# Output gates' weight tiles split two deep into two rings; LN1's second transposes moved forward, residual offset added in the second chunk

## The chip, the cores and the metric

The kernel runs on one core of a Trainium2 chip. The metric is the device time of one execution in microseconds (us); the kernel before takes 890.56 us, the median of three runs (889.98 to 890.59).

## The reference, cut to what matters

One layer of a decoder with a batch of 1, 512 tokens, a model width of 1024 and a hidden width of 4096, all in fp32. A token mixer runs gated linear attention (GLA, 4 heads, chunks of 64 tokens) and latent attention (MLA, 8 heads) side by side, merges them by sigmoid gates and projects the sum. Then comes a squared-ReLU MLP. Each half is a residual step followed by a LayerNorm, with alpha = 2^0.25:

```
h  = layer_norm(x, ln_in)
q_g, k_g, v_g, r_g, a_lr, q_lat, kv_lat, gate_logits = split(h @ w_in)
y_gla = (rms_norm(o_gla) * silu(r_g)) @ w_o_gla
y_mla = merge_heads(o_mla) @ w_o_mla
mix = (g_gla * y_gla + g_mla * y_mla) @ w_out
h1  = layer_norm(alpha * h + mix, ln1)            # LN1
ff  = square(relu(h1 @ w_ff1)) @ w_ff2
out = layer_norm(alpha * h1 + ff, ln2)
```

The change touches r_g (the output gates of GLA, a product of 512 x 1024 by 1024 x 1024), LN1, and alpha * h1, which enters LN2. Since h1 = n * g + b for the normalised rows n, the residual is n * (alpha g) + alpha b: one multiply by a row and one add of a row (the "offset").

## The kernel before, in words

**Products.** Every fp32 number that enters TensorE is split in two: hi, its rounding to the type fp32r, and lo, the rest. A product is the sum of three matmuls, hi by hi, hi by lo and lo by hi (L245 to L247 in gemm_fm, L279 to L281 in gemm_tm). In gemm_fm the weights stand still and the activations stream through, so the lo part of the weights (wlo) is used by every third matmul.

**Weights.** All weights pass through one list, `stream`, in the order of use. An entry is a tile of 128 x 1024 numbers, 512 KB. `fetch` issues an entry's DMA on SP's queue, two entries ahead, into one of three buffers named wraw. `pump` splits it: hi on ACT (L189, an activation that copies), lo on DVE (L190, a subtract). An entry is split at most "ahead" entries before its use (1 if nothing else is said), into the rings that its "home" names: "w" is two whi and two wlo buffers, "r" is two of the three wraw buffers, "a" is the large pool. A ring's buffer can be written again only when the matmuls that read its last content are through.

**Order.** Each engine works its instructions off in order and waits for semaphores of the others. The order is set when the program is built: work that runs beside the products is written as generators (`spawn`, `tick`, `finish`), and a list scheduler with estimated costs then orders each engine's instructions. `tc.issue_after(x)` ties the instructions inside it to stand behind x in that order; where x is on another engine it adds a wait.

**Output gates (proj_r, L701 to L761, 145 to 184 us).** The product is computed by a Strassen-like scheme with seven products, in the order 11, 21, t2, t1, t3, 22, t4 (RW), each with two halves of its inner dimension: 14 tiles of `stream`, 12 matmuls of 128 x 512 each (L746 to L748). The tiles 11, 21 and 22 are loaded by SP into wraw. The t tiles are sums of weights that are formed in DRAM-to-SBUF loads (r_load, and r_acc on POOL's queue, which adds in the DMA); they stand in buffers named wq and are split from there ("src"). The last, t4, is made by r_acc4 (L763), two accumulating DMAs on POOL's queue, issued after the t1 product. The sums of activations are loaded as xr tiles by SP (x_load, L709). The levels of the GLA run beside the product as generators: POOL multiplies into rp (L786, L787), ACT takes an exponential (E, L792), DVE a mask product (M, L794), and PE small matmuls (L848, L852, L856).

**LN1 (L1340 to L1357, about 545 to 570 us).** ln_rows (L422) gets mean and variance of a row block on DVE, the power -1/2 on POOL (L428), and normalises on DVE (L434, the "affine"). ln_transpose (L436) then handles a half of the tokens (256) in eight steps k: two PE transposes (L443), hi on ACT (L446), and lo on DVE (L450 and L451) or, for odd k, with ACT's help (L448). The first product behind it is f1 of the MLP. For its first weight block it runs over the first token half alone (L1356: eight steps k, each with four groups of three matmuls of 256 columns), while the second half goes through ln1(1); the second token half follows.

**The MLP (from L1507).** The hidden width is worked in four chunks. In a chunk, f1 (gemm_fm, weights in tiles of two k each, so four tiles a block) makes the hidden activations, with ReLU (L1516) and square (L1521) on ACT. win_hid (L1420) makes sums of them, and win_f2 (L1438) multiplies with w_ff2 by a Winograd-like scheme (matmuls L1454 to L1456). Its results are copied to "ev" tiles on ACT (L1471) and added to the residual in SBUF by accumulating DMAs on POOL's queue (res<-ev, L1473). The weights of w_ff2 for the next chunk are loaded on POOL's queue too (win_load, L1393), and their sums T1, T3 and T2 are formed on DVE (win_sums, L1402, operations at L1407). These are tied behind the last ev (st["ev"]), which in the first chunk does not exist yet, so that they are free there.

**The residual (residual1, L1359).** It is spawned after the first block of f1 in the first chunk. ACT's queue loads the two rows ln1_g and ln1_b, broadcast over 128 partitions (bc, 512 KB each, L106). DVE scales both by alpha (L1363, L1364), and then multiplies (L1365, L1369) and adds (L1370) for each of the four row blocks res0 to res3. All of that ends before the first chunk's win_f2 (`finish(t_r1)`).

Of the kernel before, what the change touches and what calls it, by code (L numbers as in the profile page):

```python
# [15 lines left out]
AF = mybir.ActivationFunctionType  # L16
ALU = mybir.AluOpType
AX = mybir.AxisListType

P = 128  # L20
T = 512
D = 1024
NT = T // P
# [12 lines left out]
ALPHA = 2.0 ** 0.25  # L36
# [16 lines left out]
def tile_hybrid_block(ctx: ExitStack, tc: tile.TileContext, I, out, dbg=None):  # L53
    nc = tc.nc
# [41 lines left out]
    act = nc.scalar.activation  # L96
    vtt = nc.vector.tensor_tensor
    vts = nc.vector.tensor_scalar
    stt = nc.vector.scalar_tensor_tensor
    gtt = nc.gpsimd.tensor_tensor  # L100
    mm = nc.tensor.matmul

    def bcast_row(name):
        t = A([P, D], F32, "bc")
        src = I[name]
        nc.scalar.dma_start(t, bass.AP(tensor=src.tensor, offset=src.offset, ap=[[0, P], [1, D]]))  # L106
        return t
# [21 lines left out]
    ident = ca[:, 0:P]  # L129
# [80 lines left out]
    def spawn(g):  # L210
        active.append(g)
        return g
# [19 lines left out]
    def part(x, i, c):  # L232
        return x[i][:, c] if isinstance(x, tuple) else x[:, i, c]

    def gemm_fm(pl, xs, n, evac, width=None, toks=slice(0, T), accs=None, guard=None):
        na = n // P
        accs = accs or [MM() for _ in range(na)]
        for k in range(pl["nk"]):
            hi, lo = weights(pl, k)
            xh, xl = part(xs[k], 0, toks), part(xs[k], 1, toks)  # L240
            first, last = k == 0, k == pl["nk"] - 1
            for a in range(na):
                c = slice(a * P, (a + 1) * P)
                o = accs[a][:, toks]
                mm(o, hi[:, c], xh, start=first, stop=False)  # L245
                mm(o, hi[:, c], xl, start=False, stop=False)  # L246
                mm(o, lo[:, c], xh, start=False, stop=last)  # L247
            if not last:
                tick(width)
        if guard:  # L250
            guard()
        if evac is not None:
            for a in range(na):
                evac(a, accs[a])
                if a == na // 2 - 1:
                    pump(pl["idx"][-1] + 1)
        tick(width)
        return accs
# [41 lines left out]
    PL = {}  # L300
# [16 lines left out]
    for op, _ in RW:  # L317
        for hf in range(2):
            PL["r"].append(len(stream))
            e = {"nk": 2, "n": T, "res": False}  # L320
            if op[0] == "t":
                e["src"] = lambda q=("r", op, hf): WQ[q]
            else:
                e["dmas"] = [(slice(0, 2), r_src(op, hf), None)]
            stream.append(e)
# [96 lines left out]
    def ln_rows(src, dst, mv, on_act=False):  # L422
        bst = S([P, 2, 6], F32, "bst")
        for j in range(2):
            nc.vector.bn_stats(bst[:, j, :], src[:, j * T:(j + 1) * T])
        nc.vector.bn_aggr(mv, bst)
        vts(mv[:, 1:2], mv[:, 1:2], LN_EPS, None, op0=ALU.add)  # L427
        gtt(mv[:, 1:2], mv[:, 1:2], mhalf[:, 0:1], op=ALU.pow)  # L428
        if on_act:
            nmr = S([P, 1], F32, "nmr")  # L430
            stt(nmr, mv[:, 0:1], -1.0, mv[:, 1:2], op0=ALU.mult, op1=ALU.mult)
            act(dst, src, AF.Identity, scale=mv[:, 1:2], bias=nmr)
        else:
            vts(dst, src, mv[:, 0:1], mv[:, 1:2], op0=ALU.subtract, op1=ALU.mult)  # L434

    def ln_transpose(rows, g, b, outs, hf, alt=False, n="h0"):  # L436
        tk = slice(hf * 256, (hf + 1) * 256)
        for k in range(NK):
            if len(outs) <= k:
                outs.append(A([P, 2, T], F32R, n) if n == "h0" else (B([P, T], F32R, n), B([P, T], F32R, n)))  # L440
            p = MM() if alt and k in (4, 5) else PX()
            for i in range(2):
                nc.tensor.transpose(p[:, i * P:(i + 1) * P], rows[2 * hf + i][:, k * P:(k + 1) * P], ident)  # L443
            tmp = B([P, 256], F32, "lnt")
            hi, lo = part(outs[k], 0, tk), part(outs[k], 1, tk)
            ha = act(hi, p[:, :256], AF.Identity, scale=g[:, k:k + 1], bias=b[:, k:k + 1])  # L446
            if (alt or n == "h1") and k % 2:
                act(tmp, p[:, :256], AF.Identity, scale=g[:, k:k + 1], bias=b[:, k:k + 1])  # L448
            else:
                vts(tmp, p[:, :256], g[:, k:k + 1], b[:, k:k + 1], op0=ALU.mult, op1=ALU.add)  # L450
            hd = vtt(lo, tmp, f(hi), op=ALU.subtract)  # L451
            if n == "h1":
                st["ln"] = (ha, hd)
            yield hd
# [466 lines left out]
    scale = HQ ** -0.5  # L921
# [418 lines left out]
    def ln1(hf):  # L1340
        for tt in (2 * hf, 2 * hf + 1):
            mv = S([P, 2], F32, "mv")
            ln_rows(res[tt], res[tt], mv)
        yield
        for k, _ in enumerate(ln_transpose(res, ln1g, ln1b, h1T, hf, n="h1")):
            if k % 2:
                yield
# [5 lines left out]
    finish(t_ln)  # L1353
    st["gates"] = st["ln"]
    t_ln = spawn(ln1(1))
    accs = gemm_fm(PL["f1", 0, 0], h1T, T, None, toks=slice(0, 256))  # L1356
    finish(t_ln)  # L1357

    def residual1():  # L1359
        bg, bb = bcast_row("ln1_g"), bcast_row("ln1_b")  # L1360
        yield
        with tc.issue_after(st["ln"][1].ins):
            vts(bg, bg, ALPHA, None, op0=ALU.mult)  # L1363
            vts(bb, bb, ALPHA, None, op0=ALU.mult)  # L1364
            vtt(res[0], res[0], bg, op=ALU.mult)  # L1365
        yield
        for tt in range(NT):
            if tt:
                vtt(res[tt], res[tt], bg, op=ALU.mult)  # L1369
            vtt(res[tt], res[tt], bb, op=ALU.add)  # L1370
            yield

# [29 lines left out]
    def win_sums(ci):  # L1402
        def held(*a, **kw):
            with ExitStack() as gates:
                if "ev" in st:
                    gates.enter_context(tc.issue_after(st["ev"].ins))
                vtt(*a, **kw)  # L1407
        for hf in range(2):
            q12 = WQ.pop((("f2", ci), ("12", hf)))
            t1 = WQ[("f2", ci), ("T1", hf)] = A([P, 2, T], F32, "T1")  # L1410
            held(t1, q12, WQ[("f2", ci), ("11", hf)], op=ALU.subtract)
            yield
            held(q12, WQ[("f2", ci), ("22", hf)], q12, op=ALU.subtract)
            WQ[("f2", ci), ("T3", hf)] = q12
            yield
            t2 = WQ[("f2", ci), ("T2", hf)] = A([P, 2, T], F32, "T2")
            held(t2, q12, WQ[("f2", ci), ("11", hf)], op=ALU.add)
            yield
# [88 lines left out]
    for ci in range(FC):  # L1507
# [19 lines left out]
        for b, w in F1[ci]:  # L1527
            if ci == 0 and b == 0:
                gemm_fm(PL["f1", ci, b], h1T, T, ev_h, toks=slice(256, T), accs=accs)
                t_r1 = spawn(residual1())  # L1530
            else:
                gemm_fm(PL["f1", ci, b], h1T, w * P, ev_h, width=2)
            if win and b == 0:
                t_ws = spawn(win_sums(ci))
        if ci == 0:
# [107 lines left out]
```

## Time and profile before

| what | value |
|---|---|
| median of 3 runs | 890.56 us (889.98 to 890.59) |
| the profiled execution | 890.77 us |
| its span (first to last instruction on the core) | 888.9 us |
| granted clock of TensorE, mean | 0.999 |
| PE, matmuls | 98% of the span, 4844 instructions |
| PEld, weight loads | 85%, 4844 |
| DVE | 71%, 1011 |
| ACT | 53%, 824 |
| POOL | 20%, 198 |
| instructions | 12959 |
| moved by DMA | 130.92 MB, mean 147 GB/s |

PE is TensorE's matmuls, PEld its weight loads (which overlap them), DVE VectorE, ACT ScalarE, POOL GpSimd, SP SyncE, which here only issues DMAs. The share is busy time over the span; it is an average over stages with different limits. A line of the timeline gives the start in us from the span's start, the duration, the engine and line, the output and inputs by their names in the program, the shape, and how many like instructions it groups; a bracket gives the idle time of the engine before it and what ended it. A group of matmuls such as "f32 x2" has one duration for the whole group. The names L245 and so on are lines of the kernel before.

### The profile page before, as it was taken

The page shows a single profiled execution, that of the slowest core. Times are in us where ns is not written, and L with a number is a line of the kernel's source. Part 1 is how long each engine was busy: PE and PEld are TensorE (multiplying, and loading weights), DVE is VectorE, ACT ScalarE, POOL GpSimd, SP SyncE. Part 2 cuts the span into 40 slices and gives each one's busy share as a digit, 9 for nine tenths or more (in the row PEclk, how much of TensorE's full clock was granted, in tenths as well). Part 3 has the DMA queues.
Part 4 walks back from the last instruction along what each step waited for, and adds up shares of the span by engine and source line. Part 5 has one row for each costly group of instructions (what it writes and reads, how often), then busy time and mean ns, then how long its engine had stood idle before and what let it go on. Part 6 is the DMA issues. An engine that isn't in the chain of part 4 may idle for free.

```text
span 888.9 us, 12959 instructions
## 1 busy us (share of the span) xinstructions
PE 870.0 (98%) x4844; PEld 757.6 (85%) x4844; DVE 629.8 (71%) x1011; ACT 468.8 (53%) x824; POOL 181.0 (20%) x198
## 2 busy tenths in 40 slices
PE   5999999999999999999999999999999999999996
PEld 5988887888899988888888888988888888889985
DVE  7859878967366745647766697887557646788865
ACT  5556666655366543535654424465457546656810
POOL 0324456725021010100000003004400520131001
PEclk9999999999999999999999999999999999999999
DMA  7995938234879433121307618005940990399312
GB/s 236 282 230 148 326 86 247 72 86 106 283 166 247 128 101 101 42 55 53 111 9 284 190 51 305 1 1 147 301 121 19 264 257 30 81 228 237 118 62 82
DMA packets 88414, 130.92 MB, mean 147 GB/s; under 512 B 8944, under 2 KB 50800, under 8 KB 88352
## 3 DMA queue, kind: packets, MB, share of 16 engines
q1 hardware_dynamic: 69120, 91.83, 32.7%
q0 software_dynamic: 17312, 34.61, 18.0%
q10 hardware_dynamic: 1920, 3.66, 1.1%
q8 instruction: 38, 0.62, 0.3%
q14 instruction: 24, 0.20, 0.1%
HBM read 108.58 MB, written 8.91 MB: 132 GB/s over the span
## 4 chain that ended last, share of the span: by engine, by line
PE 93%; POOL 2%; DVE 2%; issue 1%; DMA 1%; ACT 1%; POOLq 0%; SPq 0%; DVEq 0%; ACTq 0%
PE mm L245 12%; PE mm L247 12%; PE mm L246 12%; PE mm L279 6%; PE mm L281 6%; PE mm L280 6%; PE mm L1174 3%; PE mm L1173 3%; PE mm L1172 3%; PE px L1454 2%; PE px L1455 2%; PE px L1456 2%; PE mm L1455 2%; PE mm L1454 2%; PE mm L1456 2%; POOL rp L786 1%
## 5 line engine op out<-in xcount | busy, mean ns | idle before, releaser
L190 DVE TENSOR_TENSOR wlo<-wraw,whi 128x1024 fp32r<-128x1024 f32 (+2 forms) x93 | 103.9, 1118 | 98.8 <-ACT whi L189 93.8
L189 ACT ACTIVATE whi<-wraw 128x1024 fp32r<-128x1024 f32 (+2 forms) x93 | 88.7, 953 | 91.9 <-PE mm L246 40.4
L245 PE MATMUL mm<-h,whi 128*128 128x512 f32 x256 | 100.0, 391 | 0.0
L246 PE MATMUL mm<-h,whi 128*128 128x512 f32 x256 | 99.8, 390 | 0.0
L247 PE MATMUL mm<-h,wlo 128*128 128x512 f32 x256 | 95.2, 390 | 0.0
L190 DVE TENSOR_TENSOR wlo<-wq,whi 128x1024 fp32r<-128x1024 f32 x44 | 54.2, 1232 | 27.5 <-ACT whi L189 27.5
L1473 POOL DMA_DIRECT2D res<-ev x42 | 37.0, 1003 | 179.8 <-ACT ev L1471 146.2
L189 ACT ACTIVATE whi<-wq 128x1024 fp32r<-128x1024 f32 x44 | 46.4, 1056 | 23.7 <-PE mm L1173 9.9
L247 PEld LDWEIGHTS mm<-h,wlo 128*128 128x128 f32 x256 | 48.0, 188 | 10.3 <-DVE wlo L190 0.4
L245 PEld LDWEIGHTS mm<-h,whi 128*128 128x128 f32 x256 | 48.1, 188 | 9.8
L246 PEld LDWEIGHTS mm<-h,whi 128*128 128x128 f32 x256 | 48.1, 188 | 9.7
L1172 PE MATMUL mm<-sh,whi 128*128 128x256 f32 x160 | 45.4, 284 | 0.0
L1174 PE MATMUL mm<-sh,wlo 128*128 128x256 f32 x160 | 45.4, 284 | 0.0
L1173 PE MATMUL mm<-sh,whi 128*128 128x256 f32 x160 | 45.3, 283 | 0.0
L189 ACT ACTIVATE xh<-wraw 128x1024 fp32r<-128x1024 f32 (+1 forms) x28 | 27.2, 982 | 28.4 <-PE mm L281 15.7
L428 POOL TENSOR_TENSOR mv<-mv,mhalf 128x1 f32<-128x1 f32 x4 | 3.3, 838 | 170.5 <-DVE mv L427 170.5
L792 ACT ACTIVATE E<-rp 128x256 f32<-128x256 f32 x64 | 26.1, 419 | 22.3 <-POOL rp L787 13.8
L190 DVE TENSOR_TENSOR xl<-wraw,xh 128x1024 fp32r<-128x1024 f32 (+1 forms) x28 | 31.3, 1129 | 9.0 <-ACT xh L189 8.9
L1516 ACT ACTIVATE relu<-mm 128x512 f32<-128x512 f32 x24 | 14.1, 595 | 41.9 <-PE mm L247 41.9
L787 POOL TENSOR_TENSOR rp<-rp 128x256 f32<-128x256 f32 x32 | 32.3, 1010 | 11.6 <-ACT q L817 8.9
L786 POOL TENSOR_TENSOR rp<-rp 128x256 f32<-128x256 f32 x32 | 29.3, 916 | 20.2 <-ACT E L792 10.8
L794 DVE TENSOR_TENSOR M<-E,qk 128x512 f32<-128x512 f32 x32 | 28.9, 907 | 5.9 <-ACT E L792 5.9
(453 smaller groups left out, 2731.7 us busy)
## 6 DMA issues: line engine op xcount, KB each, us to landing
wraw<-in_w_ff_dram SPq DMA_DIRECT2D x36, 512.0 KB, 5.1
wraw<-in_w_in_dram SPq DMA_DIRECT2D x33, 512.0 KB, 4.0
wq<-in_w_ff_dram POOLq DMA_DIRECT2D x26, 512.0 KB, 9.7
res<-ev POOLq DMA_DIRECT2D x42, 256.0 KB, 10.0
wq<-in_w_in_dram SPq DMA_DIRECT2D x16, 512.0 KB, 6.2
wq<-in_w_in_dram POOLq DMA_DIRECT2D x16, 512.0 KB, 8.9
hsd<-hs SPq DMA_DIRECT2D x16, 256.0 KB, 4.1
xr<-hsd SPq DMA_DIRECT2D x16, 256.0 KB, 4.9
```

What stands on the lines that cost most here:

```text
L189: st["ins"] = act(hi[:, :nk, :n], raw[:, :nk, :n], AF.Copy)
L190: st["lo"] = vtt(lo[:, :nk, :n], raw[:, :nk, :n], f(hi[:, :nk, :n]), op=ALU.subtract)
L245: mm(o, hi[:, c], xh, start=first, stop=False)
L246: mm(o, hi[:, c], xl, start=False, stop=False)
L247: mm(o, lo[:, c], xh, start=False, stop=last)
L279: mm(o, xh, hi[:, :n], start=opens, stop=False, skip_group_check=share)
L280: mm(o, xh, lo[:, :n], start=False, stop=False, skip_group_check=share)
L281: mm(o, xl, hi[:, :n], start=False, stop=last, skip_group_check=share)
L786: gtt(Rv[:, :, 0, :], Rv[:, :, 0, :], Pv[:, :, 1, s - 1:s].to_broadcast([P, n, s]), op=ALU.add)
L1172: mm(oa, hi[:, k, c], xh, start=opens and k == 0 and a == 0, stop=False, skip_group_check=True)
L1173: mm(oa, hi[:, k, c], xl, start=False, stop=False, skip_group_check=True)
L1174: mm(oa, lo[:, k, c], xh, start=False, stop=k == 3, skip_group_check=True)
```

## The change

It has four parts.

1. **Output gates.** The 14 entries of r in `stream` get "ahead" 2 in place of 1, and a home of their own from the string `wwwwrwrwrwwwrw`: the first halves of t2, t1, t3 and t4 (entries 4, 6, 8 and 12) are split into two wraw buffers, all others into whi and wlo as before. The numbers of buffers stay.
2. **LN1's second transposes.** gemm_fm gets an argument `behind`. For the first block of f1 over the first token half, the matmuls of the steps k = 6 and 7 are tied behind the transposes of step k = 3 of the second token half, so that the first eight of the second half's sixteen transposes stand ahead of the last 24 matmuls.
3. **The residual's offset.** residual1 keeps only ln1_g: one load, one scale and four multiplies. A new generator, offset1, is spawned in the second chunk (ci = 1) after the first block of f1. It loads ln1_b on ACT's queue, scales it by alpha on ACT instead of DVE, and adds it to the four row blocks on DVE. In between, the first chunk's win_f2 has added its results into the same row blocks by DMA.
4. **The sums of the first chunk.** win_sums is now tied in the first chunk too: behind the last affine of LN1 (ln_rows returns it, st["aff"]).

```diff
-    def gemm_fm(pl, xs, n, evac, width=None, toks=slice(0, T), accs=None, guard=None):
+    def gemm_fm(pl, xs, n, evac, width=None, toks=slice(0, T), accs=None, guard=None, behind=None):
...
-            for a in range(na):
-                c = slice(a * P, (a + 1) * P)
-                o = accs[a][:, toks]
-                mm(o, hi[:, c], xh, start=first, stop=False)
-                mm(o, hi[:, c], xl, start=False, stop=False)
-                mm(o, lo[:, c], xh, start=False, stop=last)
+            with ExitStack() as gates:
+                if behind and k >= behind[0]:
+                    gates.enter_context(tc.issue_after(st[behind[1]].ins))
+                for a in range(na):
+                    c = slice(a * P, (a + 1) * P)
+                    o = accs[a][:, toks]
+                    mm(o, hi[:, c], xh, start=first, stop=False)
+                    mm(o, hi[:, c], xl, start=False, stop=False)
+                    mm(o, lo[:, c], xh, start=False, stop=last)
...
-            e = {"nk": 2, "n": T, "res": False}
+            e = {"nk": 2, "n": T, "res": False, "ahead": 2, "home": "wwwwrwrwrwwwrw"[2 * RW.index((op, _)) + hf]}
...
-            vts(dst, src, mv[:, 0:1], mv[:, 1:2], op0=ALU.subtract, op1=ALU.mult)
+            return vts(dst, src, mv[:, 0:1], mv[:, 1:2], op0=ALU.subtract, op1=ALU.mult)
...
-                nc.tensor.transpose(p[:, i * P:(i + 1) * P], rows[2 * hf + i][:, k * P:(k + 1) * P], ident)
+                t = nc.tensor.transpose(p[:, i * P:(i + 1) * P], rows[2 * hf + i][:, k * P:(k + 1) * P], ident)
+            if k == 3:
+                st["tr"] = t
...
-            ln_rows(res[tt], res[tt], mv)
+            st["aff"] = ln_rows(res[tt], res[tt], mv)
...
-    accs = gemm_fm(PL["f1", 0, 0], h1T, T, None, toks=slice(0, 256))
+    accs = gemm_fm(PL["f1", 0, 0], h1T, T, None, toks=slice(0, 256), behind=(6, "tr"))
...
     def residual1():
-        bg, bb = bcast_row("ln1_g"), bcast_row("ln1_b")
+        bg = bcast_row("ln1_g")
         yield
         with tc.issue_after(st["ln"][1].ins):
             vts(bg, bg, ALPHA, None, op0=ALU.mult)
-            vts(bb, bb, ALPHA, None, op0=ALU.mult)
             vtt(res[0], res[0], bg, op=ALU.mult)
         yield
+        for tt in range(1, NT):
+            vtt(res[tt], res[tt], bg, op=ALU.mult)
+            yield
+
+    def offset1():
+        bb = bcast_row("ln1_b")
+        yield
+        act(bb, bb, AF.Copy, scale=ALPHA)
+        yield
         for tt in range(NT):
-            if tt:
-                vtt(res[tt], res[tt], bg, op=ALU.mult)
             vtt(res[tt], res[tt], bb, op=ALU.add)
             yield
...
-                if "ev" in st:
-                    gates.enter_context(tc.issue_after(st["ev"].ins))
+                gates.enter_context(tc.issue_after(st["ev" if "ev" in st else "aff"].ins))
                 vtt(*a, **kw)
...
+            if ci == 1 and b == 0:
+                spawn(offset1())
             if win and b == 0:
                 t_ws = spawn(win_sums(ci))
```

In the changed kernel the lines that come after an insertion have higher numbers: 3 more from L245 on, 5 more from L446 on, and 10 to 12 more in the MLP.

## The prediction

> **What bounds the kernel now.** I read the page first (shares, then the chain), then the waits of PE, then the stages in which they fall.
>
> ```profile
> PE 870.0 (98%) x4844; PEld 757.6 (85%) x4844; DVE 629.8 (71%) x1011; ACT 468.8 (53%) x824; POOL 181.0 (20%) x198
> PE 93%; POOL 2%; DVE 2%; issue 1%; DMA 1%; ACT 1%; POOLq 0%; SPq 0%; DVEq 0%; ACTq 0%
> ```
>
> PE is busy for 98% of the span and carries 93% of the chain that ends last. So an edit counts only where PE stands still: it takes such a stand away, or it makes a new one. The waits of PE say where it stands (us in total, times, longest):
>
> ```profile
> PE mm L747 <- DVE wlo L190: 1.5, 3, 0.7
> PE mm L746 <- ACT whi L189: 0.3, 1, 0.3
> PE mm L245 <- ACT h L446: 0.3, 1, 0.3
> ```
>
> Left out are the wait at the start and one of 0.4 us behind it, which the change leaves alone. The first two rows are the output gates (proj_r), where a matmul waits for the split of its weight tile. The last is LN1. Nothing else is left to win: all gains together are under 4 us of 890.77 (the profiled execution; the sums below are made against it and then moved to the median 890.56, 0.21 lower). About 0.2%, 1.8 us, is what a measurement of this kernel can tell from no change.
>
> **Part 1, the gates' weights split two ahead.** The four stands in the timeline of PE, and the splits that end the second one:
>
> ```profile
> 149.32 0.51 PE L747 MATMUL mm<-wlo,xr 128*128 128x512 f32 x1 [0.27 <-DVE wlo L190]
> 152.70 0.73 PE L746 MATMUL mm<-whi,xr 128*128 128x512 f32 x2
> 153.95 0.50 PE L747 MATMUL mm<-wlo,xr 128*128 128x512 f32 x1 [0.52 <-DVE wlo L190]
> 173.38 0.73 PE L746 MATMUL mm<-whi,h 128*128 128x512 f32 x2 [0.34 <-ACT whi L189]
> 175.45 0.50 PE L747 MATMUL mm<-wlo,h 128*128 128x512 f32 x1 [0.72 <-DVE wlo L190]
> ```
> ```profile
> 151.59 1.05 ACT L189 ACTIVATE whi<-wq 128x1024 fp32r<-128x1024 f32 x1
> 152.68 1.22 DVE L190 TENSOR_TENSOR wlo<-wq,whi 128x1024 fp32r<-128x1024 f32 x1 [2.13 <-ACT whi L189]
> ```
>
> The brackets sum to 0.27 + 0.52 + 0.34 + 0.72 = 1.85 us. A pair that stood takes 0.73 (173.38) where a free one takes 0.61 (646.09, in part 3's rows), so four refills of the pipeline add 4 x 0.11 = 0.45. At 152.70 the hi split (151.59 + 1.05 = 152.64) also ends last though no bracket shows it, some 0.25 by estimate. Together 2.55. In the changed order both splits of the tiles after the first one stand a whole tile earlier (12 matmuls, 2.7 us at the 0.227 of part 3's rows: 24 from 646.09 to 651.53), so those stands go. The first is the exception: the lo split of t1's first half still stands on DVE behind the M (L794) that the chain POOL rp -> ACT E -> DVE M delivers, and that chain is itself held back about 1 us, because POOL now issues one r_acc4 load between two rp operations and waits there for an earlier lo split. I keep half of that stand: 2.4 us gained. Bounds: 0.8 (only the second stand goes) and 2.9 (with small gaps that no bracket shows).
>
> What this costs elsewhere: the same ACT and DVE work, only sooner. PE's lead could be given back one head later, if the rp chain didn't move with it. But that chain is paced by PE:
>
> ```profile
> 189.03 0.38 ACT L895 ACTIVATE osq<-px 128x256 f32<-128x256 f32 x1 [4.40 <-PE px L893]
> 190.49 0.80 POOL L787 TENSOR_TENSOR rp<-rp 128x256 f32<-128x256 f32 x1 [6.72 <-ACT q L817]
> ```
>
> POOL waits 6.72 us for ACT's q, which stands on ACT behind an operation that waits 4.40 us for PE. An earlier PE pulls the chain forward, and the lead stays.
>
> On SP three weight loads move behind the xr loads: the two halves of tile 22 and the first of v's second half. The 22 tiles now need the buffers that t2 and t1 occupy, so they are issued only when PE is through with those (my walk: about 151 and 157.5) instead of long before.
>
> ```profile
> wraw<-in_w_in_dram SPq DMA_DIRECT2D x2, 512.0 KB, 3.6
> wq<-in_w_in_dram SPq DMA_DIRECT2D x16, 512.0 KB, 6.2
> ```
>
> With 3.6 us to land (the row of 151 to 160 us) and 1.05 + 1.22 for the splits they are ready at about 157 and 163.5, some 1.2 us ahead of need. Cost taken: 0.
>
> **Part 2, LN1's transposes ahead, and the window sums behind the affine.** Timelines of PE, ACT and DVE:
>
> ```profile
> 560.26 1.03 PE L443 MATMUL px<-ca,res 128*128 128x128 f32 x8
> 561.62 0.74 PE L245 MATMUL mm<-h,xh 128*128 128x256 f32 x4 [0.33 <-ACT h L446]
> 562.20 0.44 PE L443 MATMUL px<-ca,res 128*128 128x128 f32 x2
> 562.66 0.39 PE L246 MATMUL mm<-h,xh 128*128 128x256 f32 x1
> 563.72 0.64 PE L245 MATMUL mm<-h,xh 128*128 128x256 f32 x4
> 564.20 0.60 PE L443 MATMUL px<-ca,res 128*128 128x128 f32 x4
> 564.55 0.36 PE L246 MATMUL mm<-h,xh 128*128 128x256 f32 x1
> ```
> ```profile
> 556.60 1.53 DVE L434 TENSOR_SCALAR res<-res,mv 128x1024 f32<-128x1024 f32 x2
> ```
>
> Four transposes and the next start take 564.55 - 564.20 = 0.35, 0.09 each. After eight from 560.26 the next matmul should start at 561.0 and starts at 561.62; after two from 562.20 at 562.4 and starts at 562.66. That is 0.6 + 0.26, 0.86 us. In the changed order 24 first-half matmuls follow the eight transposes, 24 x 0.12 = 2.9 us (four take 0.48 from 563.72 to 564.20) of cover for ACT and DVE. The transposes come 2.9 us sooner, at 557.4, and need the affine sooner too. They get it: the two window sums (L1407) that stood ahead of it now stand behind it, so it ends near 556.9 (as soon as POOL's two pow operations let it) instead of 558.1. Those sums stand between the lo parts (L451) on DVE instead, 1.14 each (635.01 to 636.15 in part 3); walked row by row every lo part still ends 0.6 us or more ahead of its matmul. Gained: 0.8. Bounds: -0.5 (a lo part late behind a sum) and 0.9.
>
> **Part 3, the offset added in the second chunk.** Off the path at first sight: four adds on DVE (1.14 each) where it has room, and on ACT a broadcast load and a scale that waits for it.
>
> ```profile
> bc<-in_ln_b_dram ACTq DMA_DIRECT2D x2, 512.0 KB, 10.0
> 609.29 1.06 ACT L189 ACTIVATE whi<-T 128x1024 fp32r<-128x1024 f32 x1 [1.13 <-DVE T L1460]
> 617.99 0.39 PE L1454 MATMUL mm<-whi,a 128*128 128x512 f32 x1
> ```
>
> In the changed order ACT issues the load near 604 and the scale stands ahead of the split at 609.29. Landing after 10.0 us, at 614, it would hold that split (after 1.0 for the scale) to 615.0 and its end to 616.1, still ahead of the matmul that uses it at 617.99. Cost 0; from about 12 us to land, what exceeds it.
>
> The adds are the matter. Between the multiplies and the adds, the first chunk's f2 accumulates into res by DMA (L1473). Before, the adds ran ahead of those DMAs; now each must wait until the last DMA into its row block has landed, and DVE waits in order. The order of DVE in the changed program from 635 us on, with what the adds wait for:
>
> ```
> wlo split, 2nd tile of chunk 1's f1
> add res0   <- landing of the 1st of the six last res<-ev DMAs
> wlo split, 3rd tile
> add res1   <- landing of the 3rd
> add res2   <- landing of the 2nd and 5th
> add res3   <- landing of the 4th and 6th
> T2 sum
> wlo split, 4th tile
> ```
>
> Before, the 2nd and the 4th of these splits and the first matmuls that use the 3rd and 4th lo part, and the six DMAs (POOL's wait for an earlier landing; issue times; landing after the issue):
>
> ```profile
> 635.01 1.22 DVE L190 TENSOR_TENSOR wlo<-wraw,whi 128x1024 fp32r<-128x1024 f32 x1
> 636.15 1.22 DVE L1407 TENSOR_TENSOR T<-wq,wq 128x1024 f32<-128x1024 f32 x1
> 646.28 1.23 DVE L190 TENSOR_TENSOR wlo<-wraw,whi 128x1024 fp32r<-128x1024 f32 x1 [4.24 <-ACT whi L189]
> ```
> ```profile
> 646.09 0.61 PE L247 MATMUL mm<-h,wlo 128*128 128x512 f32 x2
> 651.53 0.62 PE L247 MATMUL mm<-h,wlo 128*128 128x512 f32 x2
> ```
> ```profile
> 637.49 0.85 POOL L1473 DMA_DIRECT2D res<-ev x1 [5.65 <-DMA res<-ev]
> ```
> ```profile
> L1473 POOL DMA_DIRECT2D res<-ev x6: 847/1151/1862, 637.5 to 642.5; - x6
> DMA to landing us min/median/max: 6.5/8.3/10.3
> ```
>
> The first lands at 637.5 + 6.5 = 644.0, the sixth at 642.5 + 10.3 = 652.8; evenly spaced the others land at 645.8, 647.5, 649.3 and 651.0. So res0 may be added at 644.0, and the 3rd tile's split runs 645.2 to 646.4, 0.3 after PE wants it. Res1 can start at 647.5, res2 at 651.0, res3 at 652.8. Then T2 at 653.9 and the 4th split from 655.1 to 656.3, and PE wants it at 651.53 (before, this split started at 646.28): 4.8 us late in all (the 0.3 is part of it). Nothing behind has room to win that back. DVE works off its rest in the next tile (some 3 us of small operations against 5.4 us that a tile lasts on PE), so it is paid once. **Cost: 4.8 us.** Bounds: 0, if the landings came 4 us sooner, and 6, if they came 1.2 later.
>
> [...]
>
> **Sum.** -2.4 - 0.8 + 4.8 = +1.6: 892.4 for a profiled execution, **892.2** for the median.
>
> **Rivals.**
>
> (A, the other side: faster.) The landings come early and the adds wait for nothing. The six DMAs end a queue that POOL has filled with the next chunk's weights; drained 4 us sooner, the blocked splits fit. Against it: POOL's own wait of 5.65 us at 637.49 for a landing, in the same queue. Then only the gains count: 890.56 - 3.2 = 887.4. Chance 0.15.
>
> (B, slower.) The stand is long enough to lower PE's clock. Clock behind the last matmul, in the windows 884 to 886 and 887 to 888.8 (PEclk is the third number from the end), and the start:
>
> ```profile
> 881.66 0.28 PE L1587 MATMUL px<-xh,hid 128*128 128x256 f32 x1
> ```
> ```profile
> 884.00:886.00 2.00, 0.00 (x0) 0.00 (x0) 1.63 (x3) 0.00 (x0) 0.22 (x1) 1.00 0.06 23
> 887.00:888.80 1.80, 0.00 (x0) 0.00 (x0) 0.00 (x0) 0.00 (x0) 0.00 (x0) 0.50 0.14 52
> ```
> ```profile
> 9.32 1.12 PE L443 MATMUL px<-ca,x 128*128 128x128 f32 x4 [9.32 <-ACT x L432]
> 12.76 0.32 PE L279 MATMUL mm<-xh,h 128*128 128x360 f32 x1
> ```
>
> The clock is halved between 886 and 887, 4.1 to 5.1 us after the last matmul ends (881.94). My stand of 4.5 lies in between. At the start four transposes take 1.12 us against 0.60 at 564.20, and the matmuls reach their steady 0.32 at 12.76, 3.4 us after the first: 3.4 us at half speed cost 1.7. So from a stand of some 4.6 us on it costs 1.7 more: 893.9. [...] Chance 0.15.
>
> (C, the first part does not do what it says.) The 22 tiles land late: with the 6.2 us of the wq row in place of 3.6 each comes 2.6 - 1.2 = 1.4 late, ACT and PE stand in order behind them, and 1.4 of the gain is lost once: 893.6. Chance 0.14.
>
> (D, half.) Landings closer together, 1.3 us apart instead of 1.76: the last at 650.5, the stand 2.4: 889.8. Chance 0.10.
>
> The forecast keeps 0.46, for 891.4 to 893.0.
>
> **Chances and range.** Slower than 892.3: B, C and 0.18 of the forecast, 0.47. Faster than 888.8: A and a little of D, 0.17. Within: 0.36. The range leaves out A and the far end of B: 888.6 to 894.2; the forecast's own is 891.4 to 893.0.
>
> **What would show it.** Right: no wait of L746 or L747 for a split except a short one of t1; no wait of L245 for h; a new wait of PE L247 for DVE wlo of about 4.5 us near 648 to 653, with DVE idle before its adds until res<-ev lands. Wrong: DVE's adds start without a wait, or the landings are under 6 us, or the 22 tiles show up as PE <- whi.

## The result, and the profile after

The changed kernel takes 893.39 us, the median of 18 runs (891.30 to 899.39), against 890.64 us for 18 runs of the kernel before (889.98 to 891.57). The ratio is 1.0043, 95% interval 1.0028 to 1.0057: slower by 2.75 us, where 1.6 was forecast. The runs of the changed kernel lie in two groups, 12 from 891.30 to 894.33 (median 892.77) and 6 from 896.49 to 899.39 (median 897.76); those of before all lie within 1.6 us. The profiled execution took 892.86 us (span 891.1, mean granted clock 0.996 where before it was 0.999), so it is one of the lower group.

The shares and the chain of the page:

```profile
PE 872.0 (98%) x4844; PEld 758.6 (85%) x4844; DVE 628.9 (71%) x1010; ACT 469.7 (53%) x825; POOL 181.8 (20%) x198
PE 79%; DMA 8%; issue 6%; DVE 5%; POOL 1%; ACT 0%; SPq 0%; POOLq 0%; DVEq 0%; ACTq 0%
```

The shares by engine say nothing; the chain does. PE's part of it falls from 93% to 79%, and DMA, 1% before, now has 8%: somewhere the end hangs on transfers. All waits of PE in the changed kernel (the first is the start):

```profile
PE px L446 <- ACT x L435: 8.7, 1, 8.7
PE mm L250 <- DVE wlo L190: 3.2, 1, 3.2
```

The waits of proj_r and of LN1 for h are gone. One wait is left, and it is new. Its surroundings on PE and on DVE:

```profile
642.68 0.39 PE L249 MATMUL mm<-h,whi 128*128 128x512 f32 x1
643.07 0.73 PE L250 MATMUL mm<-h,wlo 128*128 128x512 f32 x2
...
648.41 0.39 PE L249 MATMUL mm<-h,whi 128*128 128x512 f32 x1
652.04 1.00 PE L250 MATMUL mm<-h,wlo 128*128 128x512 f32 x2 [3.24 <-DVE wlo L190]
652.84 0.63 PE L248 MATMUL mm<-h,whi 128*128 128x512 f32 x1
```
```profile
640.65 1.22 DVE L1381 TENSOR_TENSOR res<-res,bc 128x1024 f32<-128x1024 f32 x1 [7.39 <-DMA res<-ev]
641.79 1.22 DVE L190 TENSOR_TENSOR wlo<-wraw,whi 128x1024 fp32r<-128x1024 f32 x1
644.19 1.23 DVE L1381 TENSOR_TENSOR res<-res,bc 128x1024 f32<-128x1024 f32 x1 [1.18 <-DMA res<-ev]
646.71 1.23 DVE L1381 TENSOR_TENSOR res<-res,bc 128x1024 f32<-128x1024 f32 x1 [1.29 <-DMA res<-ev]
648.37 1.23 DVE L1381 TENSOR_TENSOR res<-res,bc 128x1024 f32<-128x1024 f32 x1 [0.43 <-DMA res<-ev]
649.63 1.23 DVE L1417 TENSOR_TENSOR T<-wq,wq 128x1024 f32<-128x1024 f32 x1
650.77 1.22 DVE L190 TENSOR_TENSOR wlo<-wraw,whi 128x1024 fp32r<-128x1024 f32 x1
```

This is the order of the forecast, line by line: four adds that each wait for the landing of an accumulating DMA, T2, and only then the split that PE wants. And the stand has a second price. A matmul that takes 0.39 at 648.41 takes 0.63 at 652.84. In windows of 0.8 us, the third number from the end is the granted clock:

```profile
652.00:652.80 0.80, 0.76 (x2) 0.63 (x3) 0.80 (x3) 0.00 (x0) 0.00 (x0) 0.71 0.00 0
652.80:653.60 0.80, 0.80 (x3) 0.66 (x2) 0.80 (x3) 0.00 (x0) 0.00 (x0) 0.50 0.53 96
...
654.40:655.20 0.80, 0.80 (x3) 0.60 (x3) 0.80 (x1) 0.80 (x1) 0.00 (x0) 0.50 0.78 277
655.20:656.00 0.80, 0.80 (x3) 0.62 (x3) 0.80 (x2) 0.15 (x1) 0.00 (x0) 0.66 0.05 18
```

The 0.71 and the 0.66 place the edges at 652.34 and 655.74: 3.4 us at half clock (a low stretch, from here on), 1.7 us lost.

A ledger follows from matmuls that are the same in both traces. One behind the gates and one ahead of the third weight tile of the second chunk, in the trace before; the first of these and the last matmul in the trace after (642.68 is above):

```profile
225.22 0.39 PE L246 MATMUL mm<-h,whi 128*128 128x512 f32 x1
...
645.87 0.39 PE L246 MATMUL mm<-h,whi 128*128 128x512 f32 x1
```
```profile
222.68 0.40 PE L249 MATMUL mm<-h,whi 128*128 128x512 f32 x1
...
883.88 0.28 PE L1599 MATMUL px<-xh,hid 128*128 128x256 f32 x1
```

Ahead of the gates the two traces are level (130.55 before, 130.53 after for the same matmuls). PE is 2.54 us ahead at 222.68, 3.19 ahead at 642.68 (645.87 before), 3.02 ahead at 643.07 (646.09 before), 0.51 behind at 652.04 (651.53 before), and 2.22 behind at the end (881.66 before). So the gates give 2.54 and LN1 0.65; the third tile's split takes 0.17, the fourth's 3.53, and the clock behind it 1.71. LN1's 0.65 has two parts: in its first half PE loses 0.31 (the last pair of transposes there starts at 544.45, 2.23 ahead of 546.68 before), and behind its second transposes it gains 0.96.

### The profile page after: what moved, and what is told of

It reads as the page before. It is cut to its first block, busy times and chain, and to the rows that moved or that the text cites. A ratio compares the mean times of both kernels' runs of the same rounds, so it can differ in the third digit from the quotient of the medians.

```text
span 891.1 us, 12966 instructions
## 1 busy us (share of the span) xinstructions
PE 872.0 (98%) x4844; PEld 758.6 (85%) x4844; DVE 628.9 (71%) x1010; ACT 469.7 (53%) x825; POOL 181.8 (20%) x198
## 4 chain that ended last, share of the span: by engine, by line
PE 79%; DMA 8%; issue 6%; DVE 5%; POOL 1%; ACT 0%; SPq 0%; POOLq 0%; DVEq 0%; ACTq 0%
PE mm L250 9%; PE mm L248 9%; PE mm L249 9%; PE mm L284 4%; PE mm L282 4%; PE mm L283 4%; PE mm L1179 3%; PE mm L1177 3%; PE mm L1178 3%; DMA res<-ev 3%; PE px L853 2%; PE px L1464 2%; PE px L1465 2%; PE px L1466 2%; PE mm L752 2%
## 5 line engine op out<-in xcount | busy, mean ns | idle before, releaser
L190 DVE TENSOR_TENSOR wlo<-wq,whi 128x1024 fp32r<-128x1024 f32 x40 | 49.6, 1240 | 27.8 <-ACT whi L189 27.7
L189 ACT ACTIVATE whi<-wq 128x1024 fp32r<-128x1024 f32 x40 | 42.2, 1056 | 24.8 <-PE mm L1178 11.9
```

What stands on the lines that cost most here:

```text
L189: st["ins"] = act(hi[:, :nk, :n], raw[:, :nk, :n], AF.Copy)
L190: st["lo"] = vtt(lo[:, :nk, :n], raw[:, :nk, :n], f(hi[:, :nk, :n]), op=ALU.subtract)
```

## The experiments

**The parts, one by one.** The first run takes the third part out again; the second makes it alone; the third keeps it, but lets the adds stand elsewhere.

e1, against the changed kernel:

```diff
     def residual1():
-        bg = bcast_row("ln1_g")
+        bg, bb = bcast_row("ln1_g"), bcast_row("ln1_b")
...
-            if ci == 1 and b == 0:
-                spawn(offset1())
```

> The changed kernel without its third part: the offset is scaled and added in the first chunk as before; the gates' rings, LN1's order and the sums behind the affine stay changed. Theory A (the adds that wait for the accumulating DMAs are all that the change costs): 887.7 us, that is 890.6 - 2.5 (gates) - 0.5 (LN1), within 0.5; runs as close together as those of before (within 1.6 us), mean granted clock 0.999, no wait of PE for wlo in the MLP. Rival B (the rings or LN1's order cost something too, or make the spread of the changed kernel's runs): above 889, or a spread of several us.

Measured: 887.36 us (886.70 to 887.44, 5 runs; 890.67 before), ratio 0.9961, interval 0.9949 to 0.9974. PE's waits hold nothing of 0.4 us or more but the start. So the other parts gain 3.3 us and cost nothing, and the third part alone turns that into a loss: 893.39 - 887.36 = 6.0.

e2, the kernel before with the third part's hunks alone:

> The kernel before with the third part alone. Theory A: PE stands about 3.4 us for the lo part of the fourth weight tile of the second chunk and then runs some 3.4 us at half clock (1.7 us): 890.6 + 5.2 = 895.8 in the common case, up to 902 in some runs, since the changed kernel's runs reach 899.4; the adds wait for res<-ev landings in the trace. Rival B (the stand comes only with the earlier start that the other parts give PE): under 893 and no such wait.

Measured: 898.05 us (895.98 to 898.97; 890.67 before), ratio 1.0079, interval 1.0065 to 1.0093. Its waits of PE, without the start, the gates and the 0.3 for h in LN1 that the kernel before has too:

```profile
PE mm L247 <- DVE wlo L190: 4.1, 2, 2.9
...
PE px L443 <- ACT lnt L448: 0.6, 1, 0.6
PE mm L246 <- DVE h L451: 0.6, 1, 0.6
```

The stand comes without the other parts, here for the third and for the fourth tile. It costs 7.4 and not 5.2: the two last rows are in LN1, a place that this part doesn't touch. That was the first sign of a second cost.

e3, the changed kernel with one tie more:

```diff
+        while "lo4" not in st:
+            yield
         for tt in range(NT):
-            vtt(res[tt], res[tt], bb, op=ALU.add)
+            with tc.issue_after(st["lo4"].ins):
+                vtt(res[tt], res[tt], bb, op=ALU.add)
...
+            if ci == 1 and b == 2:
+                st["lo4"] = st["lo"]
```

> The changed kernel with its third part kept, load and scale on ACT included, but the four adds tied behind the lo split of the fourth weight tile of the second chunk, so that no split that PE needs soon stands behind a wait for a DMA. Theory A: by then all six DMAs have landed, the adds wait for nothing, 887.7 within 0.5, and the runs lie close together. Rival C (what costs is the four adds themselves, 4.6 us of DVE, or ACT's load and scale): 892 or more, wherever the adds stand.

Measured: 886.92 us (886.86 to 887.47), ratio 0.9960, interval 0.9948 to 0.9973. The adds on DVE:

```profile
654.54 4.62 DVE L1384 TENSOR_TENSOR res<-res,bc 128x1024 f32<-128x1024 f32 x4
```

Four in a row without a wait, and no wait of PE for wlo. The same adds, load and scale that cost 6 us cost nothing 14 us later: the price is the waiting in DVE's order, not the work.

**The stand's size: how late do the landings come?** e6 halves the traffic ahead of the six accumulating DMAs (it leaves out half of the second chunk's w_ff2), e9 adds to it.

```diff
-                nc.gpsimd.dma_start(t, w2[:, k0:k0 + 3:2, j * T:(j + 1) * T])
+                if ci == 1:
+                    nc.gpsimd.memset(t[:, 1], 0.0)
+                    nc.gpsimd.dma_start(t[:, 0], w2[:, k0, j * T:(j + 1) * T])
+                else:
+                    nc.gpsimd.dma_start(t, w2[:, k0:k0 + 3:2, j * T:(j + 1) * T])
```

> The changed kernel, but the eight loads of w_ff2 for the second chunk, which stand ahead of the six accumulating DMAs in POOL's queue, bring 256 KB each in place of 512 KB (the other half of each tile is set to zero on POOL, so half of the second chunk's w_ff2 is left out). Theory A (the landings wait for that queue to drain): the last of the six lands about 4 to 8 us sooner against PE, the stands go, 887.5 within 1, runs close together. Rival F (an accumulating DMA takes its 6 to 10 us whatever stands ahead of it): landings and stands as in the changed kernel, 893 with its spread.

```diff
+        if ci == 1:
+            for c in range(2):
+                nc.gpsimd.dma_start(B([P, T], F32, "more"), w2[:, c, :T])
```

> The changed kernel with two more loads of 256 KB, which nothing reads, in POOL's queue ahead of the last six accumulating DMAs. In this build all four adds stand behind the third tile's split and T2 behind the fourth, so that a stand ahead of the third tile can't come and the fourth split follows the last add at once. Theory A (the queue's rest sets the landings): at the 206 GB/s that the traces show there, 512 KB are 2.5 us; the last landing comes about 2.5 us later against PE, the stand is 3.2 + 2.5 - 1.2 = 4.5 us, with one or two low stretches of the clock: 887.2 + 4.6 + 1.7 = 893.5, or 895.2. Rival F (landings set by each DMA alone): stand 3.2 - 1.2 = 2.0 us and no or one low stretch, 889.2 to 890.9.

Measured: e6 887.40 us (886.66 to 888.34; 890.50 before), e9 894.88 us (894.70 to 900.76, 5 runs; 890.63 before). In e6 the last two adds and the fourth split:

```profile
642.35 2.49 DVE L1381 TENSOR_TENSOR res<-res,bc 128x1024 f32<-128x1024 f32 x2 [0.24 <-DMA res<-ev]
644.88 1.23 DVE L1421 TENSOR_TENSOR T<-wq,wq 128x1024 f32<-128x1024 f32 x1
646.02 1.22 DVE L190 TENSOR_TENSOR wlo<-wraw,whi 128x1024 fp32r<-128x1024 f32 x1
```

The last add and the split are 4.8 us earlier in the trace than in the changed kernel, and PE doesn't wait for wlo. DVE's order is not quite the same: in e6 two adds, not one, stand ahead of the third tile's split. In e9 the last add and PE's wait:

```profile
650.91 1.23 DVE L1381 TENSOR_TENSOR res<-res,bc 128x1024 f32<-128x1024 f32 x1 [2.28 <-DMA res<-ev]
```
```profile
PE mm L250 <- DVE wlo L190: 4.3, 1, 4.3
```

The last add is 2.5 us later (650.91 against 648.37), as 512 KB at the expectation's 206 GB/s would have it (the changed kernel's trace moves 200 to 217 GB/s from 638.6 to 645.7 us), and the wait is 4.3 us where 4.5 was expected. The clock is low from 651.13 to 657.96, 6.8 us. So in these runs the time of the landings moved with what stands in POOL's queue: 4.8 us sooner with half of the 4 MB, 2.5 later with 512 KB more. What changes little is the time of a DMA from issue to landing (medians 8.5 and 7.1 us): the rows of issue and landing of the changed kernel, with POOL's wait ahead of the first, then of e6:

```profile
634.23 4.36 POOL L1483 DMA_DIRECT2D res<-ev x5 [7.49 <-DMA res<-ev]
...
L1483 POOL DMA_DIRECT2D res<-ev x6: 847/948/1212, 634.2 to 639.2; - x6
...
DMA to landing us min/median/max: 6.4/8.5/9.1
```
```profile
L1487 POOL DMA_DIRECT2D res<-ev x6: 850/1380/2249, 629.2 to 634.6; - x6
...
DMA to landing us min/median/max: 6.0/7.1/9.0
```

Each takes its 6 to 9 us in both, so the rival was right on that; but in e6 the first of the six is issued 5.0 us sooner and the last 4.6, since POOL itself waits for earlier landings before it issues more (7.49 us in the changed kernel, 3.4 in e6).

**The clock.** e4 makes stands on purpose, on the kernel of e1, by writing a lo split several times:

```diff
-                st["lo"] = vtt(lo[:, :nk, :n], raw[:, :nk, :n], f(hi[:, :nk, :n]), op=ALU.subtract)
+                for _ in range(1 + e.get("again", 0)):
+                    st["lo"] = vtt(lo[:, :nk, :n], raw[:, :nk, :n], f(hi[:, :nk, :n]), op=ALU.subtract)
```

> The kernel of the first of these runs, with seven stands of PE made on purpose: the lo split of the second weight tile of a block of f1 is written again 4, 5, 6, 7, 6, 5 and 8 more times (1.14 us each) in seven blocks of the second and third chunk. With about 4 us of room the stands should be some 0.5, 1.7, 2.8, 4, 2.8, 1.7 and 5 us. Theory D (the clock falls at a fixed time after the last matmul, between 4.1 and 5.1 us as behind the end of the kernel before): only the longest one lowers the clock. Theory E (the clock is set by windows of a fixed length, about 3.4 us, that run on whatever PE does): some stands of 2.8 to 4 us lower it and others don't, each low stretch lasts a whole number of windows, and the edges of all low stretches lie a whole number of windows apart. Time about 887.7 + 18 + 1.7 for each fall.

Measured: 917.50 us in one run, where two falls would have made some 909. The stands didn't take the sizes meant, since splits further on came late too, but there are enough of them. Three of the longest, and the clock around the two that lowered it and at the end:

```profile
728.07 0.50 PE L249 MATMUL mm<-h,whi 128*128 128x512 f32 x1 [2.72 <-ACT whi L189]
```
```profile
788.43 0.50 PE L1462 MATMUL px<-wraw,h1p 128*128 128x512 f32 x1 [2.39 <-ACT h1p L111]
```
```profile
807.93 0.79 PE L1462 MATMUL mm<-whi,xh 128*128 128x512 f32 x1 [2.28 <-ACT ev L1479]
```
```profile
728.00:729.40 1.40, 1.27 (x5) 0.75 (x5) 1.40 (x3) 0.01 (x1) 1.40 (x3) 0.99 1.05 177
729.40:731.00 1.60, 1.60 (x4) 1.32 (x5) 1.57 (x2) 0.00 (x0) 1.38 (x2) 0.50 1.06 175
731.00:732.80 1.80, 1.80 (x5) 1.43 (x5) 1.76 (x2) 0.00 (x0) 0.00 (x0) 0.51 1.08 132
732.80:734.00 1.20, 1.20 (x6) 0.95 (x6) 0.13 (x1) 0.00 (x0) 0.00 (x0) 1.00 0.90 221
...
807.90:811.30 3.40, 3.37 (x8) 2.69 (x9) 2.23 (x2) 3.40 (x5) 1.71 (x2) 0.50 1.04 291
811.30:813.00 1.70, 1.70 (x8) 1.39 (x8) 1.70 (x3) 1.70 (x3) 0.06 (x1) 1.00 0.87 153
913.00:913.70 0.70, 0.00 (x0) 0.00 (x0) 0.00 (x0) 0.00 (x0) 0.00 (x0) 0.99 1.03 392
913.70:915.00 1.30, 0.00 (x0) 0.00 (x0) 0.00 (x0) 0.00 (x0) 0.00 (x0) 0.50 0.06 21
```

A stand of 2.39 us left the clock alone, one of 2.28 lowered it: length doesn't decide. The low stretches begin at 729.40, 807.90 and 913.70; the distances are 78.5 and 184.3 us. Each ended stretch lasts 3.4 here, and 3.41 in e2, e5 and e12; 78.5 / 23 and 184.3 / 54 are both 3.413. So in these traces the clock goes by windows of 3.41 us whose edges the stands don't move, and a stand counted by how much of one window it filled. Theory D falls, E holds. The window before 729.40 (from 725.99) was idle for 2.14 us of its 3.41, that before 807.90 (from 804.49) for 2.24. The stand of 2.39 was cut by an edge at 787.43 into 1.39 and 1.00. The other traces agree: with windows laid on their edges, 2.0 us of idle PE in one window were enough (e10 below, 647.9 to 651.3), and 1.8 were not (e11, 655.5 to 658.9; e4 behind its last matmul, 906.9 to 910.3). In e10 the window from 654.7 was low as well, with PE idle for only 0.9 us of the low one ahead of it. Where between these the limit lies was not measured.

**The gates and LN1 by themselves.** e7 is the kernel before with the first part's one line, e8 with the second and fourth part.

> The kernel before with the first part alone (gates' weight tiles split two ahead into two rings). Theory A: 890.6 - 2.4 = 888.2, within 0.4; no wait of proj_r's matmuls for a split except a short one. Rival C (the 22 tiles land late and give 1.4 back): 889.6, and PE waits for whi in the tiles of 22.

> The kernel before with the second and fourth part (LN1's transposes and the window sums behind the affine), the offset added in the first chunk as before. Theory A: 890.6 - 0.7 = 889.9, between 889.6 and 890.2; the two stands behind LN1's second transposes are gone, and some 0.3 us comes up ahead of LN1's first transposes, as in the changed kernel's trace at 543 us. Rival: the lo parts come late behind the sums and nothing is gained, 890.6 or more.

Measured: e7 888.68 us (11 runs, 887.63 to 889.67; 890.50 before), ratio 0.9979, interval 0.9970 to 0.9987; PE's only wait in proj_r is this:

```profile
PE mm L747 <- DVE wraw L190: 0.2, 1, 0.2
```

No wait for whi: the 22 tiles are in time. e8 889.49 us (11 runs, 889.09 to 890.19), ratio 0.9989, interval 0.9980 to 0.9998. So 1.8 and 1.0 us, 2.8 together, of e1's 3.3. The 0.3 us that was expected ahead of LN1's first transposes doesn't come up in e8: PE is 0.69 ahead of before at the first pair of them behind 540 us (543.01 against 543.70) and 0.69 ahead at the last (545.99 against 546.68). What it belongs to is seen below.

**The upper group.** Five further runs and three single runs of the changed kernel, unaltered:

> The changed kernel once more, unaltered, for a second profile and for the spread of its runs. Theory A (the price is the landing of the accumulating DMAs plus low stretches of the clock of 3.41 us): runs fall in two groups, about 891 to 894 and 896 to 899, and a profile from the upper group shows landings 2 to 4 us later, a stand for the third tile's split as well or a longer one for the fourth, and two low stretches in place of one. Rival (the upper group comes from another stage): the same stand and clock in the second chunk, and the time lost elsewhere.

> The changed kernel unaltered, one profile: with a chance of about one third it falls in the upper group of its runs (896 to 899). If so, theory A expects landings later by 2 to 4 us, a longer stand and two low stretches; the rival expects the same second chunk as in the first profile and a loss elsewhere. If not, 891 to 894 with one stand of 3 to 3.5 us and one low stretch.

> As the look before: an execution of the upper group would show where its 4 us more are; one of the lower group shows one stand of 3 to 3.5 us and one low stretch of 3.41 us.

> As the two looks before: upper group (896 to 899) with a longer stand and two low stretches, or lower group (891 to 894) with one of each.

Measured: e5 893.79 us (5 runs, 892.82 to 894.99); e10 894.19, e12 892.61, and e11 896.55, one of the upper group. e5, e10 and e12 show the second chunk's stands (3.5 to 3.7 us, 0.4 to 0.8 of it for the third tile) and a low stretch of one window or, in e10, of two. In e11 the second chunk is no worse, 3.5 us of stands, and by luck of the windows without any low stretch (the clock is 1.00 from 649.0 to 658.4, and by its mean over the run, 0.996, none follows): an edge at 655.5 cuts its longer stand (the row at 657.32) into 1.0 and 1.8. Its 4 us are elsewhere:

```profile
PE mm L250 <- DVE wlo L190: 3.5, 2, 2.9
PE px L446 <- ACT lnt L453: 3.4, 1, 3.4
...
657.32 0.73 PE L250 MATMUL mm<-h,wlo 128*128 128x512 f32 x2 [2.86 <-DVE wlo L190]
```
```profile
543.66 1.06 ACT L189 ACTIVATE whi<-wraw 128x1024 fp32r<-128x1024 f32 x1 [5.82 <-DMA wraw<-in_w_ff_dram]
...
545.07 0.55 ACT L453 ACTIVATE lnt<-px,cb 128x256 f32<-128x256 f32 x1
```

A split on ACT waits 5.82 us for a load of w_ff1; behind it in ACT's order stand the evictions of LN1's transposes, and PE waits for those. The clock is low from 546.30 to 549.70. The rival of e5's expectation, a loss in another stage, holds. What makes the load late is seen where SP and POOL issue, in e11:

```profile
533.74 0.37 SPq L174 DMA_DIRECT2D wraw<-in_w_ff_dram  x1
```
```profile
533.52 0.78 POOL L1410 DMA_DIRECT2D wq<-in_w_ff_dram  x1 [2.93 <-PE mm L283]
```

POOL starts its eight loads of 512 KB for the first chunk just then, and SP's load comes 0.22 us behind the first. Before, SP's is 1.57 us ahead:

```profile
534.90 0.37 SPq L174 DMA_DIRECT2D wraw<-in_w_ff_dram  x1
```
```profile
536.47 0.78 POOL L1399 DMA_DIRECT2D wq<-in_w_ff_dram  x1 [5.68 <-issue]
```

SP's lead (POOL's issue minus SP's, us) goes with ACT's wait for that load, in the profiles of before and of every kernel that has no scale of ln1_b in residual1:

| kernel | lead | ACT waits |
|---|---|---|
| before | 1.57 | 0.39 |
| e3 | 0.87 | 1.29 |
| e12 | 0.78 | 2.23 |
| e10 | 0.76 | 1.86 |
| e6 | 0.75 | 1.23 |
| e5 | 0.65 | 2.38 |
| e9 | 0.53 | 2.73 |
| changed kernel | 0.32 | 2.58 |
| e2 | 0.26 | 2.72 |
| e16 (below) | 0.13 | 5.64 |
| e11 | -0.22 | 5.82 |

In the other profiles, whose residual1 still has that scale (e1, e4, e7, e8, e13, e14, e15), the lead is 1.16 to 2.04 and the wait at most 0.56. The waits that e2 has in LN1 and the 0.31 of the changed kernel's ledger come with waits of ACT of 2.72 and 2.58. No run moved the lead alone below 1.17, so that the lead makes the wait is argued from this table and not shown by itself.

The third part has to do with it through the order of DVE: with one scale of 1024 columns taken out of residual1, the scheduler has put DVE's operations ahead of LN1 in another order. Of the three xl splits whose buffers SP waits for, the first now stands ahead of the first affine, and some operations of the stage ahead of it have changed places too. Four runs take this apart. e13 loads and scales ln1_b in residual1 as before and moves only the adds, which brings DVE's old order back:

```diff
     def residual1():
-        bg = bcast_row("ln1_g")
+        bg, bb = bcast_row("ln1_g"), bcast_row("ln1_b")
+        st["bb"] = bb
...
+            vts(bb, bb, ALPHA, None, op0=ALU.mult)
...
     def offset1():
-        bb = bcast_row("ln1_b")
-        yield
-        act(bb, bb, AF.Copy, scale=ALPHA)
+        bb = st["bb"]
```

> The changed kernel, but ln1_b is loaded and scaled in residual1 as before (on DVE); only the four adds are moved to the second chunk. In this build DVE's order in LN1's first half is that of the kernel before again (the first affine ahead of the first xl split), and three adds stand ahead of the third tile's split, one behind it. Theory G (the upper group of the changed kernel's runs comes from LN1: the xl split ahead of the affine makes SP's third load of w_ff1 late, among POOL's eight loads): median 893 to 896 from the two stands in the second chunk, runs within 3 us of each other, no upper group, no wait of ACT's split for that load. Rival (the upper group is a matter of the second chunk's stands): a third of the runs 3 to 5 us above the others again.

e14 is e13 with e3's tie:

> As the run before, with the four adds tied behind the lo split of the fourth weight tile as well: both costs mended. Theory A with G: 887.0, between 886.5 and 887.6, runs within 1 us. If it isn't below the changed kernel without its third part (887.36), the third part gains nothing by itself.

e15 is e1 with the first affine tied behind the first xl split:

> The first of these runs (the offset in the first chunk; 887.36) with a single exchange on DVE: in LN1's first half the first xl split (1.2 us) stands ahead of the first affine, as it does in the changed kernel; nothing else differs in any engine's order. Theory G: SP's loads of w_ff1 are issued about 1 us later, the third lands 3 us or more later, PE waits some 0.3 us for LN1's transposes in the common case (887.7), and in about a third of the runs 3 to 5 us more (890 to 893). Rival (the upper group needs the stands of the second chunk): 887.4 with runs within 1 us.

e16 is e3 once more:

> The third of these runs once more (adds behind the fourth split, DVE's order in LN1 as in the changed kernel). Theory G: 887.0 in most runs, but one run in three or four 3 to 5 us above, which the five runs of the first time did not show. Rival: all runs within 1 us again.

Measured (890.50 before): e13 893.31 us (893.01 to 893.99, 5 runs), one stand of 4.2 us in the second chunk (for the third tile), one low stretch, no wait of PE in LN1 (lead 2.00, ACT waits 0.46). e14 887.77 us (887.01 to 888.44, 5 runs), ratio 0.9968, interval 0.9956 to 0.9979, a little over what was expected; no wait of ACT for the load (lead 1.16). e15 886.63 us (886.43 to 888.14, 5 runs), lead 1.17, ACT waits 0.56: no upper group, against theory G's expectation. e16 886.97 us in the median of 12 runs, but 891.87, 892.50 and 893.05 in three of them; the profile is of the 892.50, and it shows all of PE's waits from 530 us to 700 us in one line:

```profile
PE px L446 <- ACT lnt L453: 3.0, 1, 3.0
```

So the upper group needs no stand in the second chunk: e16 has none and has the group. The two profiles that fell in the group, e11 and e16, have the long wait for the load (5.82 and 5.64); no other profile is above 2.73. What is shown is that the late load goes with the scale's removal from residual1: ACT waits 1.23 to 5.82 us in the ten profiles without that scale, at most 0.56 in the eight with it. That the upper group goes with it too rests on fewer runs: none in the ten of e13 and e14, and none in the ten of e1 and e15, which keep the scale as well, against 3 of the 17 of e3 and e16; by these counts alone it could still be chance. Not shown: that the one exchange of e15 does it. That exchange takes 0.4 us of SP's lead (1.58 in e1) and no more; the kernels with the scale taken out have lost 0.7 to 1.8. The other exchanges were not tried singly.

## Why the prediction was right in kind and short in size

- **Part 1, -2.4:** right. The trace gives -2.54, e7 -1.8 in the median; the stands went, t1's first lo split kept a wait of 0.2, and the 22 tiles were in time (rival C didn't come).
- **Part 2, -0.8:** right (e8, -1.0; 0.96 behind the second transposes in the changed kernel). LN1 as a whole gives only 0.65 there: its first half lost 0.31, which e1 and e8, whose ACT doesn't wait for the load, do not lose.
- **Part 3, the mechanism of the adds:** right, instruction by instruction (e1, e2, e3). The first add was expected at 644.0 in the time of before and came at 640.65 + 3.19 = 643.84; the last was expected at 652.8 and came at 648.37 + 3.02 = 651.39, since no landing took more than 9.1 us where 10.3 was taken for the last. So the term of 4.8 was too large: it measured 0.17 + 3.53 = 3.70, nearly half of the way to rival D.
- **Part 3, the clock: the step that failed.** "So from a stand of some 4.6 us on it costs 1.7 more" made a threshold of the one fall that the trace of before shows, and so the sum has the clock at nothing. It measured 1.71: the stand of 3.24 already paid it, and so did those that filled 2.0 us of one window (e10) and 2.14 and 2.24 (e4). With the clock the cost is 5.4; that this is near the 4.8 is luck, since two errors cancel in part. What e4 shows in place of that threshold is windows of 3.41 us, 23 and 54 of them between the edges, of which one with PE at work for 1.27 us was followed by half clock.
- **What no step had, the second failure:** ACT's wait in LN1, a term that the sum has at nothing. The forecast walked DVE's order from 635 us on and took it as unchanged in LN1's first half; but with one operation taken out of residual1, others moved there. This is the upper group as far as the profiles of e11 and e16 show it: without it the median would be that of the lower group, 892.77, 0.6 above the forecast 892.2 and inside the forecast's own 891.4 to 893.0, which 893.39 is not.
- **Rival A** fell by its premise: the queue drained early enough only where its traffic was halved (e6).

Moving the offset gains nothing by itself: e1, without it, takes 887.36, e14, with it mended, 887.77. The best of these are e1 and e15, which leave the offset where it was: 887.36 and 886.63 in five runs each, too few to tell them from each other or from the medians of e3 and e16, and without an upper group.

## What to carry to other kernels

An operation that needed a DMA's landing, put into the order of an engine that also feeds TensorE, cost TensorE all of its wait that the feeds behind it had no room for (here a stand of 3.24 us, and none once the adds stood behind the fourth split, e3); look first for what stands behind it in that order, and tie it behind the feeds. Price a stand of TensorE with the clock: in these runs it ran at half speed for the next 3.41 us where 2.0 us (e10) or more of one window had been idle, and at full speed behind 1.8 (e4). And when an operation is taken away from a scheduled engine, compare the new order well ahead of the place of the change: what it releases or delays on the DMA queues is part of the price (in e11, 3.4 us and a low stretch).

## What the runs showed of the hardware that was not expected

- A load of 512 KB on SP's queue that was issued 1.57 us before a burst of eight such loads on POOL's queue landed in 5.5 us (the kernel before: issued 534.90, the split that waits for it starts at 540.43); issued 0.22 us behind its start, in 9.9 us (e11: issued 533.74, the split starts at 543.66). Between the two lies a difference in issue of under 2 us.
- An accumulating DMA of 256 KB into SBUF took 6.0 to 9.0 us to land with half of the traffic ahead of it (e6) and 6.4 to 9.1 with all of it (the changed kernel); POOL waited up to 7.5 us for an earlier landing before it issued the next.
- Low stretches of the clock lasted one window of 3.41 us (e2, e5, e12) or two (6.83 in e9 and e10), and by their position stands of nearly the same length cost 0 (e11's second chunk, 2.9 us), 1.7 (the first profile, 3.2) or 2.9 us more (e10, 3.0: low from 651.30 to 658.10, of which PE worked from 652.21 on).
